# The four RWKV pairs of a hybrid block side by side, in units of two chunks

## The chip, the cores and the metric

The kernel runs on one core of a Trainium2 chip. The metric is the device time of one execution in microseconds (us). The times of the kernel before are the median, the least and the greatest of three executions; the profile is from a further execution of the same program. Five engines work side by side and wait for each other by semaphores: TensorE (PE; its weight loads are listed as PEld), VectorE (DVE), ScalarE (ACT), GpSimd (POOL) and SyncE (SP), which here issues most loads and stores.

## The reference, cut to what matters

The block is feed-forward network, mixer, feed-forward network on 1024 tokens of width 1024, all in fp32. The mixer adds four heads of gated linear attention (GLA) and eight heads of RWKV-7:

```python
x = x + 0.5 * swiglu(rms_norm(x, ffn1_norm), ffn1_w_gate, ffn1_w_up, ffn1_w_down)   # d_ff 2816
proj = rms_norm(x, mix_norm) @ w_in
o_gla  = gla_mixer(...)     # 4 heads, dk 64, dv 128, chunks of 64
o_rwkv = rwkv7_mixer(...)   # 8 heads of 64
x = x + concatenate([o_gla, o_rwkv]) @ w_out
x = x + 0.5 * swiglu(rms_norm(x, ffn2_norm), ffn2_w_gate, ffn2_w_up, ffn2_w_down)
return rms_norm(x, final_norm)

def rwkv_step(state, inp):              # lax.scan over the tokens, for every head
    r_t, w_t, k_t, v_t, a_t, b_t = inp
    sa = einsum('bhvk,bhk->bhv', state, a_t)
    state = state * w_t + sa * b_t + v_t * k_t       # outer products of v and k
    return state, einsum('bhvk,bhk->bhv', state, r_t)
# then: group norm over each head, * ln_w + ln_b, + (sum(r*k*r_k) * v), * g
```

## The kernel before, in words

**Tiling and stages.** The tokens are two halves, A and B, of 512. Each half goes through first network, projection, mixers, output projection `pout` and second network. Every large fp32 product is three matmuls on pieces of 128x512: the weights are loaded into `raw`, ScalarE makes the rounded part `wH` (L452) and VectorE the rest `wL` (L453), and TensorE adds high by high, high by low and low by high.

**The mixers** of a half have many small, dependent matmuls. So their matmuls are interleaved with large ones of the other half's networks, the "filler": tiles `pgu` (gate and up) and `pdn` (down). `mixers()` (from L1211) writes TensorE's order by hand. Each piece of mixer work is a generator that issues its instructions up to a `yield` with an estimate of how long its result takes (table `LAT`, times `SLACK`); until that much work was issued on TensorE, fillers are issued. Between the mixers' last matmuls and `pout` stands what is left of the filler's share. The other engines work in the order in which their instructions were issued.

**RWKV.** Two heads make a pair, which fills 128 partitions; there are four pairs, and eight chunks of 64 tokens in a half. `rwkv_duo` (L49) does two pairs:
- preparation, for all eight chunks at once: load `AR` and `BK` (L62, L65), gram matmuls `pg`, masked into `WA` and `W` (L83); then the inverse of a triangular matrix by 15 triples of VectorE operations on the tile `lb` and `R` (L105 to L107), its transpose `D` (L114), matmuls `p` with `D`, `p1b`, `p`, `p2b`, and `pav`;
- the chunk loop, eight steps, each dependent on the one before: `pz`, `Z`, `pu`, `UV`, `px`, new state `X`, and the output `py`;
- the norm of all eight chunks, transposes `pyT` (L47), eight ScalarE operations (L238), two loads, and a store to the scratch `d_mix` (L242).

The second duo begins after the first one's loop. GLA is done for two heads at a time by `gla_unit` (L244): loads `cum`, `k`, `q`, `kN`, `qx`, `vN` (L252, L254), matmuls `pkv`, levels `pA` and `pB`, and `po`. The first GLA unit may start when the first duo has its loads, the second when the first is done and the duo's loop begins.

**After the mixers** `outprep` loads all of `d_mix` into `xnL` (L1271), ScalarE makes the high part `xnH` (L1272), and `pout` begins.

Of the kernel before, what the change touches and what calls it, by code (L numbers as in the profile page):

```python
# [48 lines left out]
def rwkv_duo(g, d, src, mixout):  # L49


    nc=g.nc; V,S,T,GP=nc.vector,nc.scalar,g.T,nc.gpsimd
    C=g.C; vec=g.vec
    QS=range(2); PS=[2*d,2*d+1]
    mt=lambda shape,tag,nm,**kw: g.mx.tile([128]+shape,F32,tag=tag,name=nm,**kw)
    ps=lambda nm: g.pa.tile([128,512],F32,tag="pa",name=nm)
    def ld(nm,q):
        t=mt([512],"s2",nm); nc.sync.dma_start(t,src[q][nm]); return t
    AR=[mt([2,8,64],"AR","AR") for q in QS]
    BK=[]  # L60
    for q in QS:
        nc.sync.dma_start(AR[q].rearrange("p x c t->p (x c t)"),src[q]["AR"])  # L62
        for i in range(2):
            BK.append(mt([4,2,64],"s2","BK"))
            nc.sync.dma_start(BK[-1].rearrange("p c y t->p (c y t)"),src[q]["BK"][:,512*i:512*i+512])  # L65
    pc=[g.pc[p] for p in PS]
    yield LAT["pre"]
    yield "A"

    fr=[slice(0,64),slice(64,128)]  # L70
    mg=C["mg"].rearrange("p (x t)->p x t",x=2)
    WA=[[mt([8,64],"WA","WA") for h in range(2)] for q in QS]
    W=[[mt([8,64],"W","W") for h in range(2)] for q in QS]
    for q in QS:
        for i in range(2):
            c4=slice(4*i,4*i+4)
            pg=[ps(f"pg{h}").rearrange("p (c x t)->p c x t",c=4,x=2) for h in range(2)]
            for c in range(4):
                for h in range(2):
                    T.matmul(pg[h][:,c],BK[2*q+i][fr[h],c].rearrange("p y t->p (y t)"),AR[q][fr[h],:,4*i+c,:],start=True,stop=True,tile_position=(64*h,0))  # L80
            for x,Wx in ((1,WA),(0,W)):
                for h in range(2):
                    V.tensor_tensor(Wx[q][h][:,c4],pg[h][:,:,x],mg[:,x:x+1,:].to_broadcast([128,4,64]),op=MULT)  # L83
            yield 0

    fl=lambda t: t.rearrange("p q c t->p (q c) t")
    c32=fl(mt([2,8,32],"i2","c32"))
    c32q=c32.rearrange("p (q c) t->p q c t",q=2)
    for q in QS:
        for h in range(2):  # L90
            for gg in range(2):
                rr=slice(64*h+32*gg,64*h+32*gg+32)
                S.copy(c32q[rr,q],WA[q][h][rr,:,32*gg:32*gg+32])
    c16=fl(mt([2,8,16],"s1","c16"))
    S.mul(c16,c32[:,:,0:16],C["mq0"])
    V.scalar_tensor_tensor(c16,c32[:,:,16:32],C["mq1"],c16,op0=MULT,op1=ADD)
    S.mul(c32[:,:,16:32],c32[:,:,16:32],C["mq0"])
    GP.memset(c32[:,:,0:16],0.0)
    R16=fl(mt([2,8,16],"s1","R16"))
    V.tensor_copy(R16,C["i16"].rearrange("p (o t)->p o t",o=1).to_broadcast([128,16,16]))  # L100
    yield LAT["c32"]
    for j in range(15):
        n=15-j
        lb=mt([16,n],"lb","lb",bufs=2,padded_shape=[128,16,16])
        V.stream_shuffle(lb,c16[:,:,j+1:16],[j]*16+[16+j]*16)  # L105
        V.tensor_tensor(lb,lb,R16[:,:,j:j+1].to_broadcast([128,16,n]),op=MULT)
        V.tensor_tensor(R16[:,:,j+1:16],R16[:,:,j+1:16],lb,op=ADD)  # L107
        if j%2: yield LAT["inv2"]-40*j

    R4=mt([2,8,32],"Rd","R"); R=fl(R4)  # L110
    S.mul(R[:,:,0:16],R16,C["mq0"])
    S.mul(R[:,:,16:32],R16,C["mq1"])
    D=fl(mt([2,8,32],"i2","D"))
    V.transpose(D.rearrange("p c t->p (c t)"),R.rearrange("p c t->p (c t)"))  # L114
    yield LAT["D"]
    qd=[slice(32*i,32*i+32) for i in range(4)]
    p1=ps("p1").rearrange("p (c t)->p c t",t=32)
    for c in range(16):
        for i,r in enumerate(qd):
            T.matmul(p1[r,c],c32[r,c,:],D[r,c,:],start=True,stop=True,tile_position=(32*i,32*i))  # L120
    X1=fl(mt([2,8,32],"i2","X1"))
    S.copy(X1,p1)
    yield LAT["m1"]
    p1=ps("p1b")[:,0:256].rearrange("p (c t)->p c t",t=16)
    for c in range(16):
        for i,r in enumerate(qd):
            T.matmul(p1[r,c],X1[r,c,:],R[r,c,16:32],start=True,stop=True,tile_position=(32*i,32*i))
    V.tensor_tensor(R[:,:,16:32],p1,R[:,:,16:32],op=ADD)
    D=mt([2,8,32],"i2","D2")
    V.transpose(D.rearrange("p q c t->p (q c t)"),R.rearrange("p c t->p (c t)"))  # L130
    yield LAT["m2"]
    yield "B"
    half=[(slice(64*h,64*h+32),slice(64*h+32,64*h+64)) for h in range(2)]
    R64=mt([2,8,64],"R64","R64")
    S.mul(fl(R64)[:,:,0:32],R,C["mg0"])
    S.mul(fl(R64)[:,:,32:64],R,C["mg1"])
    p2=ps("p2").rearrange("p (q c t)->p q c t",q=2,c=8)
    for q in QS:
        for c in range(8):
            for h,(ra,rb) in enumerate(half):  # L140
                T.matmul(p2[rb,q,c,:],WA[q][h][ra,c,32:64],D[ra,q,c,:],start=True,stop=True,tile_position=(64*h,64*h+32))
    X2=mt([2,8,32],"i2","X2")
    for ra,rb in half:
        S.copy(X2[rb],p2[rb])

    WN=[[mt([8,64],"WN","WN") for h in range(2)] for q in QS]
    UV=mt([2,8,2,64],"UV","UV")
    for q in QS:
        for h in range(2):
            nc.sync.dma_start(WN[q][h].rearrange("p c d->p (c d)"),src[q][f"wn{h}"])  # L150
            kr=slice(64,128) if h==0 else slice(0,64)
            nc.sync.dma_start(UV[kr,h,:,q,:],src[q]["vt"][kr].rearrange("p (c d)->p c d",c=8))
    idn=C["idn"]
    yield LAT["x2"]
    p2=ps("p2b").rearrange("p (q c t)->p q c t",q=2,c=8)
    for q in QS:
        for c in range(8):
            for h,(ra,rb) in enumerate(half):
                T.matmul(p2[ra,q,c,:],X2[rb,q,c,:],R4[rb,q,c,:],start=True,stop=True,tile_position=(64*h+32,64*h))
    for ra,rb in half:  # L160
        S.copy(R64[ra,:,:,32:64],p2[ra])
    yield LAT["pav"]
    AV=mt([8,2,64],"AV","AV")
    for q in QS:
        pav=ps("pav")
        for c in range(8):
            for h in range(2):
                kr=slice(64-64*h,128-64*h)
                T.matmul(pav[fr[h],64*c:64*c+64],WA[q][h][kr,c,:],UV[kr,h,c,q,:],start=True,stop=True,tile_position=(64-64*h,64*h))
        S.copy(AV[:,:,q,:],pav.rearrange("p (c d)->p c d",c=8))  # L170
    yield "P"
    yield LAT["w"]

    YS=AV
    X=[g.X[p] for p in PS]
    two=lambda t: t[:,0:128].rearrange("p (q d)->p q d",q=2)
    def yout(c,X):
        py=two(ps("py"))
        for q in QS:
            for h in range(2):  # L180
                T.matmul(py[fr[h],q],AR[q][fr[h],0,c,:],X[q][fr[h]],start=True,stop=False,tile_position=(64*h,64*h))
            for h in range(2):
                T.matmul(py[fr[h],q],W[q][h][:,c,:],UV[:,h,c,q,:],start=False,stop=True,tile_position=(0,64*h))
        S.copy(YS[:,c],py)
    for c in range(8):
        pz=two(ps("pz"))
        for q in QS:
            for h in range(2):
                T.matmul(pz[fr[h],q],AR[q][fr[h],1,c,:],X[q][fr[h]],start=True,stop=True,tile_position=(64*h,64*h))
        Z=mt([2,64],"Z","Z",bufs=2); V.tensor_tensor(Z,pz,AV[:,c],op=ADD)  # L190
        if c: yout(c-1,Xo)
        yield LAT["z"]
        pu=two(ps("pu"))
        for q in QS:
            for h in range(2):
                T.matmul(pu[fr[h],q],R64[fr[h],q,c,:],Z[fr[h],q],start=True,stop=True,tile_position=(64*h,64*h))
        V.tensor_copy(UV[0:64,0,c],pu[0:64])
        S.copy(UV[64:128,1,c],pu[64:128])
        XP=[mt([64],"XP","XP",bufs=2) for q in QS]
        for q in QS: S.mul(XP[q],X[q],pc[q][:,c:c+1])  # L200
        yield LAT["u"]
        px=two(ps("px"))
        for q in QS:
            for h in range(2):
                T.matmul(px[fr[h],q],WN[q][h][:,c,:],UV[:,h,c,q,:],start=True,stop=True,tile_position=(0,64*h))
        Xn=[mt([64],"X","Xn",bufs=4) if c<7 else g.st.tile([128,64],F32,tag=f"X{p}",name="Xe",bufs=2) for p in PS]
        for q in QS: V.scalar_tensor_tensor(Xn[q],px[:,q],pc[q][:,c:c+1],XP[q],op0=MULT,op1=ADD)
        Xo=X; X=Xn
# [1327 lines left out]
```

## Time and profile before

| | us |
|---|---|
| median of 3 executions | 2178.34 (2177.96 to 2182.11) |
| profiled execution | 2179.36 |
| its span | 2177.5 |
| its mean granted clock of TensorE | 0.979 |
| mixer stage of half A, from the first filler behind the projection to `pout` | 745.59 to 1021.40 |
| mixer stage of half B | about 1292.8 to 1568.1 |

An engine's busy time is the sum of its instructions; the idle time ahead of an instruction is put down to what released it. The granted clock is given as a share of full speed. Times along the rows are us from the start of the span, durations of single instructions are ns where the heading of the view says so.

### The profile page before, as it was taken

The numbers are of one execution on the slowest core, as the hardware profiler recorded it, in microseconds if no ns is written. First come the engines' busy times: TensorE is split into PE (matmuls) and PEld (weight loads), VectorE is DVE, ScalarE is ACT, GpSimd is POOL, SyncE is SP. The second block draws the span as 40 slices with busy tenths as digits, with TensorE's granted clock in tenths as the row PEclk, the third lists the DMA queues.
The fourth block names the chain that finished last, engine by engine and source line by source line (L and its number), as shares of the span: only waits on it lengthen the run. The fifth ranks groups of instructions, "written<-read, shape, count | busy, mean of one in ns | idle before, by whom it ended". The sixth has DMA issues, their size and how long they took to land.

```text
span 2177.5 us, 36074 instructions
## 1 busy us (share of the span) xinstructions
PE 2069.3 (95%) x13588; PEld 1643.8 (75%) x13588; DVE 1436.5 (66%) x2771; ACT 912.9 (42%) x1723; POOL 468.6 (22%) x489
## 2 busy tenths in 40 slices
PE   8999999979999989997999999999799999998998
PEld 7778788767788877675878887777587778876886
DVE  6665687739569575665475957566558557876755
ACT  5432233322556444343265645434344223432243
POOL 0410355445012200000001220001103035445400
PEclk9999999989999999999999999999899999998999
DMA  5333244666455823334236673333434333459542
GB/s 190 126 119 95 102 146 150 249 261 216 149 190 195 274 75 112 127 99 154 94 125 198 196 266 90 111 126 105 168 104 145 100 109 123 173 178 353 180 141 77
DMA packets 152286, 336.81 MB, mean 155 GB/s; under 512 B 25616, under 2 KB 27696, under 8 KB 152112
## 3 DMA queue, kind: packets, MB, share of 16 engines
q1 hardware_dynamic: 126976, 250.08, 35.0%
q0 software_dynamic: 21536, 73.41, 9.2%
q10 hardware_dynamic: 3600, 11.01, 1.4%
q8 instruction: 107, 1.75, 0.3%
q14 instruction: 67, 0.55, 0.1%
HBM read 242.17 MB, written 92.27 MB: 154 GB/s over the span
## 4 chain that ended last, share of the span: by engine, by line
PE 86%; DVE 5%; DMA 3%; issue 2%; ACT 2%; POOL 1%; SPq 0%; ACTq 0%; POOLq 0%; DVEq 0%
PE pgu L44 22%; PE pju L44 17%; PE pdn L44 13%; PE pp L44 11%; PE pjd L44 6%; PE pout L44 4%; PE pv L44 2%; PE py L44 1%; PE po L44 1%; DVE x L888 1%; DVE wL L453 1%; PE pt L47 1%; PE pz L44 1%; PE ptn L47 1%; PE pg L44 1%
## 5 line engine op out<-in xcount | busy, mean ns | idle before, releaser
L453 DVE TENSOR_TENSOR wL<-raw,wH 128x512 fp32r<-128x512 f32 (+1 forms) x430 | 301.0, 708 | 280.7 <-ACT wH L452 272.8
L452 ACT CAST wH<-raw 128x512 fp32r<-128x512 f32 (+1 forms) x430 | 264.0, 619 | 464.4 <-PE pgu L44 146.4
L44 PE MATMUL pgu<-xnL,wH 128*128 128x512 f32 (+1 forms) x784 | 309.9, 396 | 0.0
L44 PE MATMUL pgu<-xnH,wH 128*128 128x512 f32 (+1 forms) x784 | 308.3, 394 | 0.0
L44 PE MATMUL pgu<-xnH,wL 128*128 128x512 f32 (+1 forms) x784 | 307.8, 393 | 0.2 <-DVE wL L453 0.2
L44 PE MATMUL pju<-T,wH 128*128 128x512 f32 x640 | 201.3, 396 | 2.4 <-ACT wH L688 2.4
L44 PE MATMUL pjd<-wH,hh 128*128 128x512 f32 x528 | 172.8, 408 | 20.9 <-ACT wH L688 20.9
L44 PEld LDWEIGHTS pgu<-xnL,wH 128*128 128x128 f32 x784 | 147.8, 189 | 33.4 <-issue 0.3
L44 PEld LDWEIGHTS pgu<-xnH,wH 128*128 128x128 f32 x784 | 147.7, 189 | 33.2 <-ACT xnH L511 0.7
L44 PEld LDWEIGHTS pgu<-xnH,wL 128*128 128x128 f32 x784 | 147.8, 189 | 32.4 <-DVE wL L453 0.4
L44 PE MATMUL pdn<-wH,hH 128*128 128x512 f32 x384 | 157.6, 412 | 8.1 <-DVE hf L661 4.5
L44 PE MATMUL pdn<-wL,hH 128*128 128x512 f32 x384 | 157.9, 412 | 1.9 <-DVE wL L453 1.9
L44 PE MATMUL pdn<-wH,hL 128*128 128x512 f32 x384 | 157.6, 411 | 1.5 <-issue 1.3
L624 DVE SCALAR_TENSOR_TENSOR x<-pdn,x 128x512 f32<-128x512 f32 x152 | 104.2, 688 | 73.2 <-PE pdn L44 71.7
L44 PEld LDWEIGHTS pju<-T,wH 128*128 128x128 f32 x640 | 120.2, 188 | 31.5 <-ACT wH L688 3.3
L44 PE MATMUL pp<-xnH,wH 128*128 128x512 f32 x352 | 140.8, 400 | 0.0
L44 PE MATMUL pp<-xnL,wH 128*128 128x512 f32 x352 | 139.2, 395 | 0.0
L44 PEld LDWEIGHTS pjd<-wH,hh 128*128 128x128 f32 x528 | 103.8, 197 | 46.2 <-ACT wH L688 21.8
L44 PE MATMUL pp<-xnH,wL 128*128 128x512 f32 x352 | 138.7, 394 | 0.0
L44 PE MATMUL pju<-T,wL 128*128 128x512 f32 x320 | 126.0, 394 | 0.0
L44 PE MATMUL pjd<-wL,hh 128*128 128x512 f32 x264 | 108.0, 409 | 6.6 <-DVE wL L689 6.6
L44 PEld LDWEIGHTS pdn<-wH,hH 128*128 128x128 f32 x384 | 73.9, 192 | 29.9 <-DVE hf L661 6.1
(395 smaller groups left out, 4104.5 us busy)
## 6 DMA issues: line engine op xcount, KB each, us to landing
raw<-in_wgu_dram SPq DMA_DIRECT2D x272, 256.0 KB, 2.7
hh<-d_hid SPq DMA_DIRECT2D x66, 512.0 KB, 4.6
d_hid<-hh POOLq DMA_DIRECT2D x62, 512.0 KB, 3.8
raw<-in_wdn_dram SPq DMA_DIRECT2D x96, 256.0 KB, 2.7
raw<-in_win_t_dram SPq DMA_DIRECT2D x88, 256.0 KB, 3.0
d_x<-x SPq DMA_DIRECT2D x20, 512.0 KB, 2.6
wdk<-in_wdn_dram SPq DMA_DIRECT2D x20, 512.0 KB, 8.4
raw<-in_w_out_dram SPq DMA_DIRECT2D x32, 256.0 KB, 2.6
```

The source lines that it names most:

```text
L44: return self.t.matmul(out,lhsT,rhs,**kw)
L47: return self.t.transpose(out,in_,idn)
L452: S.copy(H, raw)
L453: V.tensor_tensor(L, raw, H.bitcast(F32), op=SUB)
L624: V.scalar_tensor_tensor(h.x[tt][:, co], ps, 0.5, h.x[tt][:, co], op0=MULT, op1=ADD)
L888: V.scalar_tensor_tensor(x, v, k, x, op0=MULT, op1=ADD)
```

## The change

`rwkv_duo` is replaced by a class `Quad`. It cuts the eight chunks of a half into four units of two chunks and works on all four pairs in each. Three generators, for preparation, loop and norm, run as streams of their own: the loop of a unit waits for the tag `P` of its preparation, the norm for the tag `L` of its loop, and the preparation of unit u for `L` and `N` of unit u-2. GLA is a fourth stream, which does both units one after the other and waits for no tag. The tiles keep their sizes with other axes (8 blocks: 4 pairs x 2 chunks) except those of the inverse, which have 8 blocks in place of 16. The scratch tensors `AR`, `BK`, `bv`, `g`, `vt`, `wn` and the RWKV part of `mix` now hold the four pairs side by side. The state of the four pairs is one tile: `Xt = px + X`, `Xn = Xt * pc`. The table `LAT` and some buffer counts change.

```diff
-LAT=dict(pre=4444,c32=1600,inv2=1750,D=1500,...,w=2115,z=1400,u=1350,x=1650,gn=14000,gpre=2635,...)
+LAT=dict(pre=3000,gram=0,c32=3000,inv2=1400,D=900,...,w=600,z=1000,u=1000,x=1500,gn=6000,gpre=2635,...)
+class Quad:
+    def prep(self):
+        for u in range(4):
+            if u>1: yield f"?L{u-2}"
+            to=slice(128*u,128*u+128)
+            AR=mt([8,128],"AR","AR")
+            nc.sync.dma_start(AR,src["AR"].rearrange("p q x t->p (q x) t")[:,:,to])
+            BK=mt([4,256],"BK","BK")
+            nc.sync.dma_start(BK,src["BK"][:,:,256*u:256*u+256])
...
+            for j in range(15):
+                n=15-j
+                lb=mt([8,n],"lb","lb",bufs=2,padded_shape=[128,8,16])
+                V.stream_shuffle(lb,c16[:,:,j+1:16],[j]*16+[16+j]*16)
+                V.tensor_tensor(lb,lb,R16[:,:,j:j+1].to_broadcast([128,8,n]),op=MULT)
+                V.tensor_tensor(R16[:,:,j+1:16],R16[:,:,j+1:16],lb,op=ADD)
+                if j%2: yield LAT["inv2"]
...
+            yield f"P{u}"
+    def loop(self):
+        for u in range(4):
+            yield f"?P{u}"
+            for c in range(2):
+                pz=four("pz")
...
+                Z=mt([4,64],"Z","Z",bufs=1); V.tensor_tensor(Z,pz,AV[:,c],op=ADD)
+                yield LAT["z"]
...
+                V.tensor_copy(UV[0:64,0,:,cs],pu[0:64])
+                S.copy(UV[64:128,1,:,cs],pu[64:128])
+                yield LAT["u"]
...
+                Xt=mt([4,64],"Xt","Xt",bufs=1); V.tensor_tensor(Xt,px,X,op=ADD)
+                V.tensor_tensor(Xn,Xt,pc,op=MULT)
...
+                S.copy(AV[:,c],py)
+                yield LAT["x"]
+            yield f"L{u}"
+    def norm(self):
+        for u in range(4):
+            yield f"?L{u}"
...
+            nc.sync.dma_start(src["mix"][:,:,to],o)
+            yield f"N{u}"
-BUFS = dict(s2=7, W=4, WA=4, WN=4, AR=2, s1=2, i2=3, g1=3)
+BUFS = dict(s2=7, W=4, WA=2, WN=4, AR=2, UV=2, AV=2, R64=2, s1=2, i2=3, g1=3, s3=2)
-        def allowed(s):
-            if s in L:
-                return "A" in R[0].tags if s is L[0] else L[0].done and "P" in R[0].tags
-            return s is R[0] or "Q" in R[0].tags
+        todo = [Stream(x) for x in (quad.loop(), quad.prep(), quad.norm(), both_gl())]
```

SyncE's queue at the start of half A's mixers, the loads of the first RWKV work and of the first GLA unit. Before:

```order
L62 DMA AR<-d_AR_0_5600 128x1024
L65 DMA BK<-d_BK_0_5612 128x512 x2
L62 DMA AR<-d_AR_0_5780 128x1024
L65 DMA BK<-d_BK_0_5792 128x512 x2
L252 DMA cum<-d_la_0_5448 128x512
L252 DMA k<-d_kk_0_6412 128x512
L252 DMA q<-d_q_0_6351 128x512
L254 DMA vN<-d_vn_5369 128x4x256
L252 DMA kN<-d_kN_0_6592 128x512
```

The same place in the changed kernel:

```order
L69 DMA AR<-d_AR_5591 128x8x128
L72 DMA BK<-d_BK_5603 128x4x256
L260 DMA cum<-d_la_0_5439 128x512
L260 DMA k<-d_kk_0_6385 128x512
L260 DMA q<-d_q_0_6325 128x512
L260 DMA kN<-d_kN_0_6562 128x512
L260 DMA qx<-d_qx_0_6328 128x512
L262 DMA vN<-d_vn_5363 128x4x256
L452 DMA raw<-in_wdn_dram 128x512 x2
```

One `AR` and one `BK` for all four pairs stand there now in place of two `AR` and four `BK` for two; `kN` and `qx` moved ahead of `vN`. On TensorE the first `pkv` stood behind 40 fillers and four groups of `pg`; it now stands behind 19 fillers alone.

TensorE at the end of half A's mixers, from the fillers ahead of the last `pyT` to `pout`. Before:

```order
L44 MATMUL pgu<-xnH,wH 128x512
L47 MATMUL pyT<-ct,AV 128x128 x8
L44 MATMUL pgu<-xnL,wH 128x512
L44 MATMUL pgu<-xnH,wL 128x512
L44 MATMUL pgu<-xnH,wH 128x512
L44 MATMUL pgu<-xnL,wH 128x512
L44 MATMUL pgu<-xnH,wL 128x512
L44 MATMUL pout_10205<-wH,xnH 128x512
```

The same place in the changed kernel, where the left-out rows are more of the same fillers, 49 in all:

```order
L43 MATMUL pdn<-wL,hH 128x512
L46 MATMUL pyT<-ct,AV 128x128 x4
L43 MATMUL pdn<-wH,hL 128x512
L43 MATMUL pgu<-xnH,wH 128x512
L43 MATMUL pgu<-xnL,wH 128x512
L43 MATMUL pgu<-xnH,wL 128x512
...
L43 MATMUL pout_10238<-wH,xnH 128x512
```

The last transposes are four, of one unit, and stand 49 fillers ahead of `pout` and not five. Over the whole mixer stage of a half the counts are the same, 648 fillers and 1344 mixer matmuls; the fillers stand in 63 separate runs and stood in 82.

## Rows read from the trace of the kernel before

**Rows 1.** The page: busy time of each engine, and the group of `wL`
```profile
PE 2069.3 (95%) x13588; PEld 1643.8 (75%) x13588; DVE 1436.5 (66%) x2771; ACT 912.9 (42%) x1723; POOL 468.6 (22%) x489
...
L453 DVE TENSOR_TENSOR wL<-raw,wH 128x512 fp32r<-128x512 f32 (+1 forms) x430 | 301.0, 708 | 280.7 <-ACT wH L452 272.8
```

**Rows 2.** Waits of PE: reader, releaser, total us, number, longest
```profile
PE pout L44 <- ACT xnH L1272: 22.4, 2, 11.4
...
PE p L44 <- DVE D L114: 7.0, 3, 3.0
```

**Rows 3.** Windows: stretch, length; PE, PEld, DVE, ACT, POOL busy; clock, DMA, GB/s
```profile
745.50:1021.50 276.00, 254.76 (x3307) 190.20 (x3305) 171.29 (x492) 121.05 (x248) 2.12 (x4) 0.97 0.38 118
1292.80:1568.10 275.30, 254.39 (x3306) 190.07 (x3305) 174.56 (x492) 120.97 (x247) 17.12 (x19) 0.98 0.38 121
761.00:783.00 22.00, 21.98 (x305) 16.75 (x307) 21.45 (x85) 13.99 (x27) 0.31 (x1) 1.00 0.44 102
783.00:788.00 5.00, 1.95 (x50) 1.35 (x44) 4.93 (x20) 1.54 (x3) 0.00 (x0) 1.00 0.18 50
1022.00:1024.00 2.00, 2.00 (x6) 1.58 (x5) 2.00 (x4) 1.80 (x4) 0.00 (x0) 0.50 1.05 397
1800.00:1900.00 100.00, 100.00 (x431) 80.85 (x430) 81.99 (x98) 39.64 (x70) 56.17 (x52) 1.00 0.44 156
```

**Rows 4.** Timeline of PE, 832 to 839: start, duration, instruction
```profile
832.80 0.50 PE L44 MATMUL pgu<-xnH,wH 128*128 128x512 f32 x1
...
835.31 0.45 PE L44 MATMUL pu<-Z,R 64*64 64x64 f32 x8
835.68 0.50 PE L44 MATMUL pgu<-xnL,wH 128*128 128x512 f32 x1
...
838.18 0.45 PE L44 MATMUL px<-UV,WN 128*64 128x64 f32 x8
```

**Rows 5.** Timeline of PE, start and end of half A's stage
```profile
745.59 0.39 PE L44 MATMUL pgu<-xnH,wH 128*128 128x512 f32 x1
...
759.98 1.09 PE L44 MATMUL pkv<-vN,kN 128*64 128x128 f32 x16
...
1008.11 1.06 PE L47 MATMUL pyT<-ct,AV 128*128 128x128 f32 x8 [0.32 <-DVE AV L226]
...
1021.40 0.80 PE L44 MATMUL pout<-wH,xnH 128*128 128x512 f32 x1 [11.06 <-ACT xnH L1272]
```

**Rows 6.** Timeline of SP's DMA issues, start and end of the stage
```profile
744.58 0.44 SPq L62 DMA_DIRECT2D AR<-d_AR  x1
...
750.27 0.55 SPq L254 DMA_DIRECT2D vN<-d_vn  x1
...
1012.63 3.20 SPq L242 DMA_DIRECT2D d_mix<-AV  x2
...
1016.42 0.94 SPq L1271 DMA_DIRECT2D xnL<-d_mix  x2
```

**Rows 7.** Timeline of ACT after the last `pyT`
```profile
1008.82 4.34 ACT L238 ACTIVATE AV<-pyT,vt 64x256 f32<-64x256 f32 x8 [2.23 <-PE pyT L47]
```

**Rows 8.** DMA issues, 744 to 760: count, KB each, us to landing
```profile
vN<-d_vn SPq DMA_DIRECT2D x1, 512.0 KB, 8.4
...
UV<-d_vt SPq DMA_DIRECT2D x1, 128.0 KB, 5.9
```

**Rows 9.** Groups of DVE by shape, 745 to 1022: busy us, mean ns, idle
```profile
L83 DVE TENSOR_TENSOR WA<-pg,ct 128x256 f32<-128x256 f32 x16 | 6.1, 419 | 3.3 <-PE pg L44 3.3
...
L105 DVE STREAM_SHUFFLE lb<-c 128x128 f32<-128x128 f32 x2 | 0.6, 308 | 0.0
...
L105 DVE STREAM_SHUFFLE lb<-c 128x64 f32<-128x64 f32 x2 | 0.5, 242 | 0.0
...
L106 DVE TENSOR_TENSOR lb<-lb,R 128x64 f32<-128x64 f32 x2 | 0.4, 220 | 0.0
L107 DVE TENSOR_TENSOR R<-R,lb 128x64 f32<-128x64 f32 x2 | 0.4, 218 | 0.0
```

More of the change, by code (lines that the diff above doesn't have):

```diff
@@ L7 @@
 MULT,ADD,SUB,MAX,MIN=ALU.mult,ALU.add,ALU.subtract,ALU.max,ALU.min
-LAT=dict(pre=4444,c32=1600,inv2=1750,D=1500,m1=1200,m2=1200,D2=1300,x2=600,pav=900,w=2115,z=1400,u=1350,x=1650,gn=14000,gpre=2635,lev0=5723,lev=1944,sc=770,on=8372)
-SEQ_MID=3
+LAT=dict(pre=3000,gram=0,c32=3000,inv2=1400,D=900,m1=900,m2=900,x2=700,pav=900,w=600,z=1000,u=1000,x=1500,gn=6000,gpre=2635,lev0=5723,lev=1944,sc=770,on=8372)
 def const_array():
@@ L47, in transpose @@
         return self.t.transpose(out,in_,idn)
[L49 to L78, printed above, removed]
-                for h in range(2):
-                    T.matmul(pg[h][:,c],BK[2*q+i][fr[h],c].rearrange("p y t->p (y t)"),AR[q][fr[h],:,4*i+c,:],start=True,stop=True,tile_position=(64*h,0))
-            for x,Wx in ((1,WA),(0,W)):
-                for h in range(2):
[L83 to L208, printed above, removed]
-        if c==SEQ_MID: yield "M"
-        yield LAT["x"] if c<7 else 0
-    yout(7,Xo)
-    yield "Q"
-    for q,p in enumerate(PS): g.X[p]=X[q]
-    c16_=YS.rearrange("p c q t->p (c q) t")
-    b16=lambda t: t.rearrange("p (c o)->p c o",o=1).to_broadcast([128,16,64])
-    sm=mt([16],"sm","sm",bufs=2)
-    V.tensor_reduce(sm,c16_,axis=AX.X,op=ADD)
-    V.tensor_scalar(sm,sm,-1.0/64,None,op0=MULT)
-    V.tensor_tensor(c16_,c16_,b16(sm),op=ADD)
-    vr=mt([16],"sm","vr",bufs=2)
-    for i in range(2):
-        sq2=mt([8,64],"s2","sq2"); S.activation(sq2,c16_[:,8*i:8*i+8],AF.Square)
-        V.tensor_reduce(vr[:,8*i:8*i+8],sq2,axis=AX.X,op=ADD)
-    g.rsqrt(g.mx,vr,vr,64,64e-5)
-    V.tensor_tensor(c16_,c16_,b16(vr),op=MULT)
-    yield LAT["gn"]
-    pyv=[]
-    for i in range(2):
-        py=ps("pyT")
-        for j in range(4): T.transpose(py[:,128*j:128*j+128],YS[:,4*i+j].rearrange("p q d->p (q d)"),idn)
-        pyv.append(py.rearrange("p (c h t)->p c h t",c=4,h=2))
-    yT=YS.rearrange("p c q t->p (c q t)").rearrange("p (q c t)->p q c t",q=2,c=8)
-    for q,p in enumerate(PS):
-        for h in range(2):
-            lw,lb_=("ln_w","ln_b") if h==q else ("ln_ws","ln_bs")
-            for i in range(2):
-                S.activation(yT[fr[h],q,4*i:4*i+4,:],pyv[i][fr[q],:,h,:],AF.Identity,scale=vec(lw,p)[fr[q]],bias=vec(lb_,p)[fr[q]])
-        o=yT[:,q].rearrange("p c t->p (c t)")
-        bv=ld("bv",q); V.tensor_tensor(o,o,bv,op=ADD)
-        gt=ld("g",q); V.tensor_tensor(o,gt,o,op=MULT)
-        nc.sync.dma_start(mixout[q],o)
@@ L270, in gla_unit @@
     D=g.mx.tile([128,2,4,32],F32,tag="D32",name="D32")
-    pA=[ps(f"pA{h}") for h in range(2)]
     def lev(h):
@@ L288, in gla_unit @@
     qe,ke=e64
+    pA=[ps(f"pA{h}") for h in range(2)]
     for h in range(2):
@@ L291, in gla_unit @@
             T.matmul(pA[h][0:64,64*c:64*c+64],ke[fr[h],64*c:64*c+64],qe[fr[h],64*c:64*c+64],start=True,stop=True,tile_position=(64*h,0))
-    yield 0
     qe,ke=e32
@@ L313, in gla_unit @@
         for h in range(2):
-            if h: yield 0
             for c in range(4):
@@ L330, in gla_unit @@
     for h in range(2):
-        if h: yield 0
         for c in range(4):
@@ L373 @@
 NH, NL, NR = 6, 6, 4
+WIDE = {f"{n}{p}": (n, p) for n in ("AR", "BK", "bv", "g", "vt") for p in range(4)} | {f"wn{p}{i}": (f"wn{i}", p) for p in range(4) for i in range(2)}
 class Pool:
@@ L425, in block_kernel @@
     GP.memset(carry, 0.0)
-    g.X, g.S, g.pc, g.el = [], [], {}, {}
-    for i in range(4):
-        t = wk.tile([P, 64], F32, tag=f"X{i}", bufs=2, name="X0")
-        GP.memset(t, 0.0)
-        g.X.append(t)
+    g.S, g.el = [], {}
+    g.X = wk.tile([P, 4, 64], F32, tag="X", bufs=2, name="X0")
+    GP.memset(g.X, 0.0)
     for i in range(2):
@@ L940, in dn @@
         def dn(nm, cols=HT):
-            return dram(f"{nm}_{hf}", [P, cols])
+            nm, p = WIDE.get(nm, (nm, None))
+            if p is None:
+                return dram(f"{nm}_{hf}", [P, cols])
+            return dram(f"{nm}_{hf}", [P, 4 * cols])[:, cols * p:cols * p + cols]
         def put(nm, t, cols=HT):
@@ L1074, in proj @@
                 S.activation(Em, cs, AF.Exp, scale=CDEC)
-                pc = wk.tile([P, 8], F32, tag=f"pc{p}", name="pc")
-                V.tensor_copy(pc, E[:, :, 64])
-                g.pc[p] = pc
+                if p == 0:
+                    g.pc = wk.tile([P, 4, 8], F32, tag="pc", bufs=2, name="pc")
+                V.tensor_copy(g.pc[:, p], E[:, :, 64])
                 r = shifted(f"r{p}", new("r"))
@@ L1213, in mixers, with wide @@
         d = lambda nm, cols=HT: dram(f"{nm}_{hf}", [P, cols])
-        def rw(k):
-            return rwkv_duo(g, k, [{n: d(f"{n}{p}", 2 * HT if n in ("AR", "BK") else HT) for n in ("AR", "BK", "vt", "bv", "g")} | {f"wn{i}": d(f"wn{p}{i}") for i in range(2)} for p in (2 * k, 2 * k + 1)],
-                            [d(f"mix{4 + p}") for p in (2 * k, 2 * k + 1)])
+        def wide(nm, cols=HT):
+            return dram(f"{nm}_{hf}", [P, 4 * cols]).rearrange("p (q t)->p q t", q=4)
+        quad = Quad(g, {n: wide(n) for n in ("bv", "g", "vt", "wn0", "wn1", "mix")} |
+                    {"BK": wide("BK", 2 * HT), "AR": wide("AR", 2 * HT).rearrange("p q (x t)->p q x t", x=2)})
         def gl(p):
@@ L1222, in gl @@
                             [d(f"go{2 * p + j}") for j in range(2)], [d(f"mix{2 * p + j}") for j in range(2)])
+        tags = set()
         class Stream:
             def __init__(self, gen):
-                self.gen, self.at, self.tags, self.done = gen, T.ns, set(), False
+                self.gen, self.at, self.wait, self.done = gen, T.ns, None, False
             def step(self):
-                self.tags.add("started")
                 try:
                     lat = next(self.gen)
-                    if isinstance(lat, str):
-                        self.tags.add(lat)
-                        lat = 0.0
+                    while isinstance(lat, str) and lat[0] != "?":
+                        tags.add(lat)
+                        lat = next(self.gen)
+                    self.wait, lat = (lat[1:], 0.0) if isinstance(lat, str) else (None, lat)
                     self.at = T.ns + lat * SLACK
@@ L1237, in step, with free, both_gl @@
                     self.done = True
-        R = [Stream(rw(k)) for k in range(2)]
-        L = [Stream(gl(p)) for p in range(2)]
-        def allowed(s):
-            if s in L:
-                return "A" in R[0].tags if s is L[0] else L[0].done and "P" in R[0].tags
-            return s is R[0] or "Q" in R[0].tags
-        todo = R + L
+            def free(self):
+                return self.wait is None or self.wait in tags
+        def both_gl():
+            for p in range(2):
+                yield from gl(p)
+        todo = [Stream(x) for x in (quad.loop(), quad.prep(), quad.norm(), both_gl())]
         filling = True
@@ L1253, in mixers @@
                     break
-                can = [s for s in todo if allowed(s)]
+                can = [s for s in todo if s.free()]
                 t0, n = T.ns, 1
@@ L1270, in outprep @@
             raw = h.xl(kt).bitcast(F32)
-            nc.sync.dma_start(raw, dram(f"mix{kt}_{h.i}", [P, HT]))
+            nc.sync.dma_start(raw, dram(f"mix{kt}_{h.i}", [P, HT]) if kt < 4 else dram(f"mix_{h.i}", [P, 4 * HT])[:, HT * kt - 4 * HT:HT * kt - 3 * HT])
             S.copy(h.xh(kt), raw)
```

155 lines of the change are left out of this document (added).

## The prediction

> **What bounds the kernel now.** I read the page first: TensorE is busy for 95% of the span, VectorE for 66%, ScalarE for 42% [rows 1]. The median of the runs shown is 2178.34 us; the profiled execution took 2179.36, its span 2177.5. Every duration below is from that execution, so the sum starts at 2179.36, and at the end I take off the 1.0 us by which it stands above the median.
>
> The change touches only the two mixer stages, so I looked at those by windows. Half A's stage takes 276.0 us with 254.76 of them busy on TensorE, half B's 275.3 with 254.39 [rows 3]. Idle are thus 21.2 and 20.9, together 42.1 us, and more than this no better order of the same work could win except by making the work itself cheaper. The waits of TensorE split it: `pout`, the output projection, waited twice for `xnH`, 22.4 us in all and 11.4 at most [rows 2]; the remaining 19.8 lie inside the stages.
>
> Where the inside waits come from is seen in two short stretches: from 761 to 783 us VectorE is busy for 21.45 of 22 us and TensorE has work all the time; from 783 to 788 VectorE is busy for 4.93 of 5 and TensorE for 1.95 [rows 3]. There TensorE has run out of what the hand-written order put ahead of the products `p` with `D`, the end of a triangular inverse that VectorE works out in 45 small operations; it is the wait of up to 3.0 us, 7.0 in three, of rows 2.
>
> **The change, part by part.** The instructions of TensorE stay the same in number: 648 filler matmuls of the other half's feed-forward network and 1344 small mixer matmuls in a half, before and after; only their order differs.
>
> *Fewer switches.* A pure filler stretch sustains 431 matmuls in 100 us at full clock, with TensorE busy throughout [rows 3], so one each 0.232 us. Ten filler matmuls between two mixer groups took 2.51 us (832.80 to 835.31, and 2.50 from 835.68 to 838.18) [rows 4], where 10 x 0.2315 is 2.32: each separate run of fillers costs about 0.2 us more than its matmuls. The order of before has 82 such runs in a half, the new one 63, so 38 fewer in the two halves: 38 x 0.2 = **-7.6 us** (0 if the extra time belongs to the small matmuls and not to the switch, -11 if 0.3 is lost with the groups' own ends).
>
> *The wait of `pout`.* Before, the last eight transposes `pyT` run at 1008.11 and only five fillers are left behind them. ScalarE takes 4.34 us for eight operations, the store `d_mix` follows at 1012.63, the loads `xnL` are issued at 1016.42, and `pout` starts at 1021.40 after 11.06 us of waiting [rows 5, 6, 7]. In the new order the last `pyT` group has four transposes, of a unit of two chunks, and 49 fillers stand behind it: 49 x 0.2315 + 0.2 = 11.5 us of cover. The path itself takes 1021.40 - 1008.11 = 13.3 before; ScalarE's eight operations have the same number but 128 columns in place of 256, which by the ratio of smaller operations in rows 9 (242 against 308) makes them 4.34 x 0.79 = 3.4, so the path is about 12.4. A wait of 0.9 us is left each time: 22.4 - 1.8 = **-20.6 us**. After the wait the granted clock was 0.50, the lower of the two levels of 1.2 and 2.4 GHz; six matmuls started in 2 us, where the 431 in 100 make 8.6 [rows 3]. That cost 2.6 x 0.23 = 0.6 us in these 2; how long it lasted the row doesn't say. Between one such stretch and four it is 0.6 to 2.4 us in a half; I take the upper part, since `pout` is followed by 192 dense matmuls that had to bring the clock back: **-4 us** for both halves (-1 to -5).
>
> *The inside waits.* VectorE's work grows by the inverse: it was 15 triples (shuffle, multiply, add) on 16 blocks, twice in a half; it is 15 triples on 8 blocks, four times. At 128x64, the size in the middle of the new ones, a triple cost 242 + 220 + 218 = 680 ns [rows 9], so a unit's inverse takes 15 x 0.68 = 10.2 us. It now lies beside loop steps and GLA of other units in place of filler alone: from a unit's last gram matmuls `pg` to its `p` the new order gives TensorE (in fillers x 0.2315 plus groups) 43, 46, 30 and 24 us in units 0 to 3. For VectorE I count there, from the new order by these rows with `wL` at 708 ns [rows 1], 27 to 30, 34, 25 and 20 to 23 us. Three units have cover, the last is at the edge. So most of the 19.8 us should go; I keep 2.5 in each half for the last unit and its two loop steps, which have only three or four fillers between dependent groups: 19.8 - 5 = **-15 us** (from 0 to -19.8).
>
> *What is late next: the start.* GLA's stream now runs from the first moment, and its `pkv` stands behind 19 fillers, not behind four `pg` groups and 40. The stage begins at 745.59, so TensorE reaches `pkv` at 745.59 + 19 x 0.2315 + 0.2 = 750.2. `pkv` needs `vN`. Before, `vN` was issued at 750.27 and took 8.4 us, to 758.7, and `pkv` ran at 759.98 [rows 5, 6, 8], with no wait. Up to and with `vN`, SyncE's queue held two `AR` of 512 KB, four `BK` of 256, `cum`, `k`, `q` of 256 and `vN` of 512, in all 3.25 MB, and these took from 744.58 to 758.7, 14.1 us. In the new order one `AR` and one `BK` of 512 KB stand there, and `kN` and `qx` beside `cum`, `k`, `q`: 2.75 MB. In proportion that is 2.2 us less, so `vN` lands between 756.5 and 758.7 (nothing gained, since the new `AR` rows are short, of 512 bytes); I take 757.3. TensorE then waits 7 us in A and, with the same order and loads, about 6.5 in B; everything else waits behind `pkv` on TensorE's queue, the fillers too. Then the clock: after 11 us of waiting it was 0.50, so I add 1.75 each. In all **+17 us** (0 if `vN` comes before TensorE, +22 if it lands no earlier than before and the clock costs 2.4 each).
>
> What short rows do is bounded by the old `UV` load, 128 KB with rows of 256 bytes, landing in 5.9 us, where whole-row loads of 512 KB took 8.4 [rows 8]: nothing strange is seen. The Trainium skill (DMA: Bandwidth & Descriptors, section Specifications) puts the least transfer at line rate at 512 bytes; by this rule the new rows are just long enough, `vN` lands at the earlier end, and the sum is 2 us lower. No row here shows a transfer of 512-byte rows.
>
> The wait is what the Trainium skill warns of (TensorE: Matmul & The Clock Gate, section HAM oscillation — how this bites in real kernels): a wait for a transfer leaves TensorE idle, and its next work begins at the slower clock. The trace agrees with 0.50 behind `pout`. By the rule the 3.5 us for the clock are in the sum; had the clock stayed full it would be 2144.5.
>
> *The rest.* The state update becomes two VectorE operations of 256 columns in place of one multiply on ScalarE and one on VectorE for each pair; a 128x256 operation from PSUM costs 419 ns [rows 9]; it is within the counts above. Uncovered, 16 steps x 0.42 are 7 us. `BK` has one buffer now, so the next unit's load waits for the `pg` of the unit before; 160 fillers (37 us) lie between the two units' `pg` in the new order, so it costs nothing, or, if SyncE's queue is held by it and the weights behind it come late, one wait of some 8 us, the landing time of `vN`. Stores to the wide scratch have the same bytes. I cost all three at nothing.
>
> **Sum.** -7.6 - 20.6 - 4 - 15 + 17 = -30.2: 2179.4 - 30.2 = 2149.2, and 2148 against the median.
>
> **Rivals.**
> - *VectorE stays the bound inside the stages.* The inverses are interleaved with steps, and the row 761 to 783 shows how full VectorE can be. Against: 66% of the span, and the counts above. The 15 us don't come: 2163.
> - *The end still waits.* The path from `pyT` to `pout` passes one SyncE queue, on which other loads stand (`raw` of `w_out` among them), and the loads `xnL` wait for all stores; if this takes as long as before in spite of 49 fillers, through a store or a load that is issued late, 20.6 + 4 stay: 2172. For it: the old path had 3.8 us between store and loads [rows 6].
> - *The start costs nothing.* `vN` and `kN` come with the lighter queue, or the stage's fillers hold TensorE longer: 2131.
> - *Slower.* The small operations of a loop step (`Z`, `UV`, `Xt`, `Xn`) queue behind inverse triples on VectorE, which works in order. Three of the dependent operations in each of 8 steps in both halves make 48 places. If each waits for one triple of 0.68 us with nothing else for TensorE to do, it is 48 x 0.68 = 33 us, just what the change wins, so this decides from one triple for each. With a `wL` of 0.71 as well it is 48 x 1.39 = 67: 2149 + 67 = 2215. Against: five to eight fillers (1.2 to 1.9 us) stand between most dependent groups.
> - *It doesn't do what it says:* TensorE has as many matmuls as before and is 95% full; what is won at the end is lost at the start. 2178.
>
> **How the numbers follow.** Forecast 0.50, its own range 2136 to 2160; VectorE bound inside 0.21; end still waits 0.11; start free 0.07; slower 0.07; nothing 0.04. Within 0.2%, 4.4 us, is what a measurement of this kernel can tell from no change. Faster: the first four, less a part of the third that falls into that band (0.04): 0.85. Same: 0.04 + 0.04 = 0.08. Slower 0.07. The range from 2130 to 2172 holds the forecast, the second and third rival, and most of the fourth.
>
> **What would show it.** Right: `pout` waits about 1 us in place of 11, the clock behind it at 1.00; `pkv` waits some 7 us near 750 and again 4.6 us after the start of B's stage, with 0.50 behind it; waits of TensorE for `D` and others inside the stages under 3 us a half; both stages near 260 us. Wrong: a stage with VectorE at 95% or more over 20 us while TensorE waits; `pout` waiting for a load; a `pkv` that runs at once; waits spread over `pz`, `pu`, `px` in the middle of the stage, which is the slower case.

## The result, and the profile after

The changed kernel takes 2147.85 us in the median of four executions (2144.43 to 2152.21); the ratio to the kernel before is 0.985, 95% interval 0.9823 to 0.9878. The forecast was 2148 us. The profiled execution is the slowest of the four, 2152.21 us with a span of 2150.4, so everything read from its trace explains a gain of 27.1 us of span (2177.5 - 2150.4), not the 32 between the medians.

The page's first line stands beside the one of [rows 1]:

```profile
PE 2056.5 (96%) x13588; PEld 1643.0 (76%) x13588; DVE 1451.6 (68%) x3031; ACT 910.6 (42%) x1703; POOL 469.0 (22%) x490
```

TensorE's matmuls are as many as before; its busy time is 12.8 us less, for the same work. (The trace lists most of the mixers' matmuls as two records each, so the 3306 of a stage are the 648 fillers and the 1344 mixer matmuls.) The windows of the two mixer stages, and behind them stretches just after a wait (columns as in [rows 3]):

```profile
744.50:1006.10 261.60, 249.40 (x3306) 190.87 (x3304) 177.49 (x619) 119.16 (x236) 3.27 (x7) 0.99 0.41 123
1277.70:1542.30 264.60, 251.88 (x3306) 192.76 (x3304) 178.96 (x619) 119.19 (x236) 7.56 (x11) 0.97 0.41 122
756.20:760.20 4.00, 3.96 (x21) 3.10 (x21) 1.88 (x6) 0.59 (x1) 0.00 (x0) 0.50 1.17 236
1290.30:1296.30 6.00, 6.00 (x37) 4.73 (x37) 1.88 (x6) 2.57 (x4) 0.00 (x0) 0.50 1.23 242
1306.60:1310.00 3.40, 3.40 (x19) 2.69 (x9) 3.40 (x14) 3.22 (x8) 0.00 (x0) 0.50 0.02 7
1006.00:1008.00 2.00, 1.95 (x5) 1.39 (x6) 1.98 (x4) 1.64 (x4) 0.00 (x0) 0.56 0.95 324
1542.30:1544.30 2.00, 2.00 (x8) 1.34 (x9) 2.00 (x4) 1.64 (x4) 0.61 (x1) 1.00 0.93 282
```

The first two stretches stand behind `pkv` in A and B, the third behind a wait of 1.0 us of GLA's `pA` in B, and the last two behind `pout` in A, where the clock is 0.56, and in B, where it is 1.00. Stage A is 14.4 us shorter than in [rows 3], stage B 10.7. Idle are 12.2 and 12.7 us, and the waits of TensorE say where (total us, number, longest):

```profile
PE pkv L43 <- DMA vN<-d_vn: 15.1, 2, 7.9
...
PE pA L43 <- DVE ke L289: 3.3, 4, 1.0
PE pout L43 <- ACT xnH L1285: 3.0, 2, 1.9
...
PE pout L43 <- DVE xnL L1286: 0.6, 1, 0.6
PE p L43 <- DVE D L130: 0.5, 2, 0.2
```

`pout` waits 3.0 us and not 22.4 [rows 2]; the wait for the inverse's `D`, 7.0 before, is 0.5; a new one stands at the top, `pkv` for `vN`, 15.1. The timeline of TensorE at both ends of half A's stage, beside [rows 5], and `pkv` of half B:

```profile
756.24 1.98 PE L43 MATMUL pkv<-vN,kN 128*64 128x128 f32 x16 [7.12 <-DMA vN<-d_vn]
...
992.20 0.60 PE L46 MATMUL pyT<-ct,AV 128*128 128x128 f32 x4
...
1006.05 0.64 PE L43 MATMUL pout<-wH,xnH 128*128 128x512 f32 x1 [1.87 <-ACT xnH L1285]
...
1290.26 1.97 PE L43 MATMUL pkv<-vN,kN 128*64 128x128 f32 x16 [7.95 <-DMA vN<-d_vn]
```

SyncE's issues in the same places, beside [rows 6], and ScalarE and VectorE after the last `pyT`, beside [rows 7]:

```profile
743.60 0.61 SPq L69 DMA_DIRECT2D AR<-d_AR  x1
...
998.55 0.57 SPq L249 DMA_DIRECT2D d_mix<-AV  x1
999.21 1.06 SPq L452 DMA_DIRECT2D raw<-in_w_out_dram  x2
1000.31 3.68 SPq L1284 DMA_DIRECT2D xnL<-d_mix  x7
```

```profile
992.83 3.72 ACT L244 ACTIVATE AV<-pyT,vt 64x128 f32<-64x128 f32 x8 [0.28 <-PE pyT L46]
...
997.84 0.69 DVE L248 TENSOR_TENSOR AV<-AV,g 128x512 f32<-128x512 f32 x1
...
1005.38 0.62 ACT L1285 CAST xnH<-xnL 128x512 fp32r<-128x512 f32 x1 [3.56 <-DMA xnL<-d_mix]
```

The path from the last `pyT` to `pout` did not get shorter: 1006.05 - 992.20 = 13.9 us, and 13.3 before. Two lines of the trace of before show why, the last store and the first use of the loads:

```profile
1015.51 0.33 SPq L242 DMA_DIRECT2D d_mix<-AV  x1
...
1020.73 2.65 ACT L1272 CAST xnH<-xnL 128x512 fp32r<-128x512 f32 x4 [6.40 <-DMA xnL<-d_mix]
```

The store is now issued 6.4 us after `pyT`, as VectorE's last operation on the tile ends (997.84 + 0.69); of the two stores of before the last went 7.4 us after `pyT`. Behind it the gain is lost: the loads `xnL` follow 1.8 us after the store, where they followed 0.9 after the last one, with two weights of `w_out` between them on SyncE's queue; and ScalarE starts on the first of them 5.1 us after its issue, where it took 4.3. What covers the path now is the 49 fillers.

### The profile page after: what moved, and what is told of

The parts are those of the page before. It is cut to its first block, busy times and chain, and to the rows that moved or that the text cites. A ratio compares the mean times of both kernels' runs of the same rounds, so it can differ in the third digit from the quotient of the medians.

```text
span 2150.4 us, 36294 instructions
## 1 busy us (share of the span) xinstructions
PE 2056.5 (96%) x13588; PEld 1643.0 (76%) x13588; DVE 1451.6 (68%) x3031; ACT 910.6 (42%) x1703; POOL 469.0 (22%) x490
## 5 line engine op out<-in xcount | busy, mean ns | idle before, releaser
L460 DVE TENSOR_TENSOR wL<-raw,wH 128x512 fp32r<-128x512 f32 (+1 forms) x430 | 296.5, 697 | 277.7 <-ACT wH L459 275.4
L696 DVE TENSOR_TENSOR wL<-s,wH 128x512 fp32r<-128x512 f32 x80 | 68.3, 855 | 42.5 <-ACT wH L695 42.5
```

The lines of the kernel that those rows point to most:

```text
L460: V.tensor_tensor(L, raw, H.bitcast(F32), op=SUB)
L696: V.tensor_tensor(L, f, H.bitcast(F32), op=SUB)
```

## The experiments

Ratios are to the kernel before, measured on the same chip with the runs; the changed kernel's is 0.985. Each has an interval of about 0.0025 to either side, 5 to 6 us, so differences of two runs below that are said from the traces or left open.

**The end by itself: the kernel before with more cover.**

```diff
-    run(f1b, n=3)      # and f2a for the other half
+    run(f1b, n=4)
```

> The kernel before with 48 more fillers of each half between its last transposes and the output projection, 53 in place of 5; everything else as before. Theory (the end's gain is cover alone and does not need the units of two chunks): pout's wait of 22.4 us falls to about 2, and with the clock behind it 22 to 24 us are won: about 2157 us, two thirds or more of what the whole change wins. Rival (only a shorter last unit shortens the path, and fillers moved ahead are missed behind pout): 2170 us or more.

2162.82 us, ratio 0.9919 (0.9893 to 0.9944). The wait of `pout` in this kernel:

```profile
PE pout L44 <- ACT xnH L1272: 5.2, 2, 3.7
```

17.2 of the 22.4 us are gone without any of the units, and about half of the whole change's gain comes with one number. The waits for `D` stay: 6.1 us. The first theory is nearer, but its two thirds are missed: 5.2 us of the wait are left, not 2, and a slow clock still follows, with 46.4 us for the 192 matmuls of `pout` in each half, where it was 46.0 and 47.3.

**The end of the changed kernel with the same edit.**

> The changed kernel with 48 more fillers of each half between the last transposes and the output projection, 97 in all. Theory (the rest of the end wait, 1.9 and 1.2 us, and the slow clock behind it, 1.7 and 1.3 us, are due to too little cover): both go, 5 to 6 us less, about 2142 us. Rival (the fillers are missed where they stood before, behind the output projection): the same wait comes back there, 2147 us, no change.

2138.07 us, ratio 0.981 (0.9785 to 0.9834), some 9 us less than the changed kernel, more than the 5 to 6 of the theory. `pout` waits no longer, and its 192 matmuls (counted from the first start to the last, and one step of 0.23 more) take 44.5 and 44.4 us, where they took 46.2 and 45.8. The fillers are not missed behind it. The stages' windows, used below:

```profile
741.10:1011.90 270.80, 260.05 (x3354) 199.93 (x3353) 185.24 (x631) 125.30 (x247) 3.27 (x7) 0.99 0.44 132
1270.60:1541.30 270.70, 259.90 (x3353) 199.91 (x3352) 185.98 (x629) 125.49 (x247) 7.88 (x11) 0.99 0.43 128
```

**The start: GLA's first products later.**

```diff
-    yield LAT["gpre"]
+    yield LAT["gpre"] if p else 9500
```

> Only the first GLA unit's estimated latency is changed (2635 to 9500), so that its first products stand behind 55 fillers and the first gram products, not behind 19 fillers. Theory (the new wait for vN, 7.1 and 7.9 us, and about 1.9 us of slow clock behind each, is a term of its own): the wait goes and nothing takes its place, 15 to 19 us less than the changed kernel, about 2130 us. Rival (VectorE is near its limit, so GLA's levels collide with unit 0's inverse when they come later): waits of TensorE for D, ke or UV inside the stages grow by as much as the start wins, 2142 to 2150 us.

2143.99 us, ratio 0.9833 (0.9809 to 0.9858): only some 4 us, not clear of the noise. The wait for `vN` is gone, and these stand in its place:

```profile
PE p L43 <- DVE D L115: 8.2, 4, 2.7
...
PE pg L43 <- DMA BK<-d_BK: 3.4, 2, 2.1
...
PE pB L43 <- issue: 2.5, 1, 2.5
```

```profile
840.00:852.00 12.00, 9.93 (x208) 7.60 (x206) 11.57 (x54) 10.08 (x24) 0.00 (x0) 1.00 0.21 67
```

```profile
913.01 3.71 ACT L244 ACTIVATE AV<-pyT,vt 64x128 f32<-64x128 f32 x8
916.74 0.40 ACT L112 ACTIVATE R<-R,ct 128x128 f32<-128x128 f32 x1
...
916.75 0.69 DVE L248 TENSOR_TENSOR AV<-AV,bv 128x512 f32<-128x512 f32 x1 [3.89 <-ACT AV L244]
```

In the 12 us before the first of these `p`, the second unit's, VectorE is busy for 11.57: there GLA's work falls onto the inverse, as the rival says, and the wait is 1.4 us in each half. The larger waits, 2.6 us in A and 2.7 in B, are the third unit's and have another cause. VectorE sits idle for 3.89 us before it, since ScalarE works on the norm of the unit before, and the two operations on `R` that `D` needs stand behind that norm's eight in ScalarE's order. So the rival's time came, but at most 2.8 of the 8.2 us by its mechanism. From this run I formed a new theory, that the wait at the start could not be won at all, and tried it without touching TensorE's order.

**The start: `vN` and `kN` loaded first.**

```diff
-    cum=ld("cum"); k=ld("k"); q=ld("q"); kN=ld("kN"); qx=ld("qx")
-    vN=...; nc.sync.dma_start(vN,...)
+    vN=...; nc.sync.dma_start(vN,...)
+    kN=ld("kN")
+    if p==0: yield "V"
+    cum=ld("cum"); k=ld("k"); q=ld("q"); qx=ld("qx")
...
+        next(todo[3].gen)      # issues these two ahead of AR and BK
```

> The changed kernel, TensorE's order untouched, with the first GLA unit's loads of vN and kN issued ahead of AR and BK; cum, k and q come 0.75 MB later. First theory (the wait of pkv is a price of its own): 13 to 19 us less, about 2131 us. Theory formed after gla_later (the start is bound by all the loads and by VectorE's work on them, and the wait only shows where TensorE meets it first): pkv runs at once or nearly so, and pg, pA and p wait together about as long as pkv did; 2142 to 2149 us.

2134.71 us, ratio 0.9797 (0.977 to 0.9825), by the ratios 11.5 us less than the changed kernel (13 by the medians). The new theory fell, the first one stands, at the lower edge of its range: most of the wait is a price of its own.

```profile
747.31 1.09 PE L43 MATMUL pkv<-vN,kN 128*64 128x128 f32 x16
751.03 1.16 PE L43 MATMUL pg<-AR,BK 64*128 64x128 f32 x16 [1.27 <-DMA BK<-d_BK]
...
762.20 0.32 PE L43 MATMUL pA<-qe,ke 64*32 64x32 f32 x4 [2.07 <-DVE ke L291]
```

`pkv` runs at once, and 3.3 us of waits for `BK` and `ke` remain in A, where `pkv` and `pA` waited 8.1. In both halves together the waits for `vN`, `BK` and `ke` fall from 18.4 to 7.4 us.

**VectorE's cover.**

```diff
                 V.stream_shuffle(lb,c16[:,:,j+1:16],[j]*16+[16+j]*16)
+                V.stream_shuffle(lb,c16[:,:,j+1:16],[j]*16+[16+j]*16)
```

> The changed kernel with each of the 15 shuffles of every inverse done twice (the second writes the same values again), about 15 x 0.24 = 3.6 us more for VectorE in each of eight units. Theory (units 0 to 2 have cover, unit 3 is at the edge): only the last unit of each half pays, 0 to 7 us, 2148 to 2155 us, with the new wait at p with D in unit 3. Rival (VectorE bounds the stages everywhere): all of it is paid, 29 us, about 2177 us.

2157.62 us, ratio 0.9899 (0.9872 to 0.9925): some 10 us of the 29 that were added (eight units at 3.6).

```profile
PE pout L43 <- ACT xnH L1286: 9.0, 2, 4.5
...
PE p L43 <- DVE D L116: 6.6, 4, 2.2
```

Between the two, nearer the first. Units 0 and 1 hide it all; in half A unit 2's `p` waits 2.1 us and unit 3's 1.1, and the end 4.5, 2.6 more than before. I had given unit 2 five us to spare; it has less than 1.5.

**No preparation ahead.**

```diff
-            if u>1: yield f"?L{u-2}"
+            if u: yield f"?L{u-1}"
```

> The changed kernel, but a unit's preparation starts only when the loop of the unit before is done, so that the inverses no longer lie beside the loop steps (the norm still does). Theory (overlap of neighbouring units is what takes away the waits inside the stages): no filler is left for unit 3, whose whole chain of inverse, two steps and norm stands bare; 30 to 40 us of waits more in each half and slow clock with them, 2210 to 2240 us, more than before the change. Rival (the gain is from units of half the size and from the norm by units alone): within 15 us of the changed kernel, below 2165 us.

2229.5 us, ratio 1.0226 (1.019 to 1.0261), slower than the kernel before, as the theory said.

```profile
PE pout L43 <- ACT xnH L1285: 20.8, 2, 11.2
PE pyT L46 <- DVE AV L233: 19.4, 4, 6.8
```

```profile
1010.00:1046.00 36.00, 17.60 (x228) 13.88 (x227) 9.70 (x27) 7.65 (x18) 0.00 (x0) 0.50 0.11 33
```

The last unit's chain stands bare: in 36 us TensorE is busy for 17.60, all of it at half clock, and VectorE for 9.70. Units of two chunks are worth nothing without their overlap. The change also set new estimates in `LAT` for the order by hand; no run separates them from the units.

**The price of a switch.**

```diff
                     T.matmul(p1[r,c],c32[r,c,:],D[r,c,:],...)
+                if c==3: yield 0        # so too in p1b, p, p2b, pav and py; and n=4 at both ends
```

> The changed kernel with 48 more fillers at each half's end (as changed_more_tail, 2138 us) and further points at which fillers may stand between a unit's small matmuls: 85 separate runs of fillers in a half, not 63, with equal matmuls. Theory (each run costs 0.2 us): 44 more runs, 9 us more than changed_more_tail, about 2147 us, and about 4 us more of TensorE's busy time in each stage. Rival (the extra time belongs to the small matmuls, not to the switch): below 2141 us.

2155.03 us, ratio 0.9891 (0.9864 to 0.9919), 17 us more than with the runs unsplit, where the theory had 9.

```profile
742.60:1020.70 278.10, 266.22 (x3353) 199.09 (x3351) 183.46 (x624) 122.35 (x241) 3.27 (x7) 0.99 0.40 118
1279.70:1557.30 277.60, 265.59 (x3354) 198.97 (x3353) 184.62 (x625) 122.35 (x241) 7.59 (x11) 0.99 0.41 119
```

For equal matmuls TensorE is busy 6.2 and 5.7 us longer than in the windows of the kernel with more tail: 11.9 / 44 = 0.27 us for each run of fillers. The rest of the 17 is in waits (1.2 us more in each stage), in `pout` (0.3 each) and outside the stages.

**Both ends together.** The changed kernel with n=4 and the first GLA unit's estimate at 6000:

> Two edits of the changed kernel together: 48 more fillers at each half's end, and the first GLA unit's latency estimate at 6000, which puts its first products behind 31 fillers and the gram products. Theory (the start is bound by loads and VectorE): the gain of the end as in changed_more_tail and at most some 4 us from the start, 2133 to 2138 us. Rival (the start wait can still be won by finding the right place): about 2125 us.

2129.17 us, ratio 0.9771 (0.9743 to 0.9799): between the two, 4 us better than its theory.

```profile
PE p L43 <- DVE D L115: 2.0, 2, 1.0
...
PE pkv L43 <- DMA vN<-d_vn: 1.1, 2, 0.8
```

With 31 fillers ahead of `pkv` and not 55, the waits for `D` are 2.0 us in place of the 8.2 of gla_later, and `vN` costs 1.1. Against changed_more_tail it is 8 to 9 us less: the start can be won by place too. With n=4 and the loads of `vN` and `kN` first:

> The changed kernel with two edits: vN and kN loaded ahead of AR and BK, and 48 more fillers at each half's end. Theory (start and end are separate terms): 13 us for the start and 7 to 10 us for the end, 2125 to 2129 us. Rival (what the start wins, the end's fillers win too): 2131 us or more.

2127.79 us, ratio 0.9769 (0.9744 to 0.9794), 9 us less than changed_more_tail by the ratios: start and end add up within the noise, and loading first is worth no more here than the right place, from which it can't be told apart. Its stages are the cleanest look at the work itself:

```profile
742.40:1006.00 263.60, 258.36 (x3354) 198.62 (x3354) 185.29 (x631) 122.63 (x245) 3.27 (x7) 1.00 0.45 136
1264.60:1529.10 264.50, 258.19 (x3355) 198.52 (x3353) 185.92 (x630) 122.94 (x245) 7.89 (x11) 1.00 0.45 131
```

With `pA` put 7 fillers later on top of that:

> The same with the first GLA unit's latency estimate at 3600, not 2635, so that pA stands 7 fillers (1.6 us) later. Theory (what is left of the start wait is pA, which waits for VectorE's ke): pA's wait of 2 us in half A goes, 0 to 3 us less than the kernel without it. Rival (it collides with the inverse of unit 0, as in gla_later): p waits for D instead, no gain or up to 3 us more.

2133.12 us, ratio 0.9792 (0.9763 to 0.9822). It is some 5 us slower: its four executions, 2131.34 to 2141.5, all lie above those without it, 2125.02 to 2128.77, on the same chip. Neither theory names what the trace shows: the order now has `pg` ahead of `pkv`, and it waits for `BK`.

```profile
PE pg L43 <- DMA BK<-d_BK: 8.7, 2, 4.6
```

## Why the prediction was right

The mechanism was right in its four parts, and the median came out as forecast; the second is partly luck, since the terms missed in both directions and the trace explains 27 us, where the sum had 30. Inside the parts some steps failed, as said below. Term by term, in us for both halves, measured in the profiled executions:

| term | forecast | measured | from |
|---|---|---|---|
| fewer switches | -7.6 | -10.3 | 38 runs x 0.27 |
| slow clock behind the inside waits | 0 | -2.5 | 4.5 before, 2.0 after; see below |
| inside waits | -15 | -13.0 | 19.8 to 6.8 (24.9 idle - 15.1 - 3.0) |
| start, wait for `vN` | +13.5 | +15.1 | waits |
| slow clock behind it | +3.5 | +5.0 | 10 us of work at 0.50 |
| wait of `pout` | -20.6 | -19.4 | 22.4 to 3.0 |
| slow clock behind it | -4 | -2.6 | 192 matmuls, 44.45 at full clock: 46.0 + 47.3 before, 46.2 in A now |
| a second wait in `pout`, B | 0 | +1.3 | 45.8 at a clock of 1.00; 0.6 for `xnL`, the rest small gaps |
| sum | -30.2 | -26.4 | span: -27.1 |

The clock terms come out of the busy times. At a clock of 1.00 throughout, the new order's work takes 258.36 + 258.19 less 96 fillers of 0.2315, 494.3 us in both stages. The changed kernel was busy for 249.40 + 251.88 = 501.3: 7.0 more. Of these 5.0 are the half clock behind `pkv`, by the windows 4 us long in A and 6 in B, and 1.7 the 3.40 us at 0.50 from 1306.6 on; the table counts all but the 5.0 to the inside waits. The kernel before was busy for 509.15 [rows 3]: 14.8 more than the work, of which 10.3 are switches at the 0.27 of split_runs and 4.5 are left. Two windows of it that I had not looked at show half clock behind the inside waits, and would cost some 4 us:

```profile
790.00:796.00 6.00, 4.45 (x50) 3.58 (x50) 3.26 (x7) 1.60 (x3) 0.00 (x0) 0.51 0.11 37
1335.00:1339.00 4.00, 3.85 (x164) 3.54 (x165) 3.37 (x9) 1.85 (x3) 0.00 (x0) 0.57 0.51 149
```

**Switches.** Mis-sized: the 0.2 was read from one interval, and split_runs has 0.27. The upper bound named there, 0.3, was nearer; whether the rest is in the ends of the small groups isn't shown.

**The inside waits.** The step held, and preparation_not_ahead shows that it needs the overlap: without it the time comes back, as waits of the last unit. The missing term is the clock: a wait was priced as idle time alone.

**The end.** The step "the path is about 12.4" failed; it is 13.9. ScalarE's eight operations take 3.72, not 3.4, a ratio that was read from VectorE's rows. The rest is behind the store, which the forecast left as it was: two weights on SyncE's queue and slower loads, 1.6 us together. This is the second rival's mechanism in small, at 0.9 us, and not at 10. The 3.8 us between store and loads that spoke for this rival were misread: the row holds two stores, and 0.9 us lie between the last and the loads. That the clock would then stay up failed in half A, where it was 0.56 behind a wait of 1.87; in half B it stayed at 1.00 behind 1.15. The larger point is that the term was right and its cause wider than the change: cover alone gives most of it.

**The start.** The place held, and nearly the size: 7.1 and 7.9 us for a forecast of 7 and 6.5. In A `pkv` starts as `vN` lands, 756.2; it took 12.6 us from the first issue for 2.75 MB, 14.1 for 3.25 before: of the 2.2 us in proportion 1.5 came. In B nothing came. The first issue of the changed kernel, then of the kernel before the first issue, that of `vN`, and its time to landing:

```profile
1276.71 1.70 SPq L69 DMA_DIRECT2D AR<-d_AR  x1
...
1291.80 0.42 SPq L62 DMA_DIRECT2D AR<-d_AR  x1
...
1297.98 0.37 SPq L254 DMA_DIRECT2D vN<-d_vn  x1
...
vN<-d_vn SPq DMA_DIRECT2D x1, 512.0 KB, 6.8
```

The changed kernel takes 13.5 us to `pkv` at 1290.26, the kernel before 13.0 to the landing at 1304.8. By the Trainium skill's least transfer at line rate (DMA: Bandwidth & Descriptors, section Specifications) rows of 512 bytes should have brought all 2.2 in both halves, by my estimate; the trace agrees to 0.7 us in A and not at all in B, and doesn't say what the rest is.

**The rivals.** VectorE as the bound didn't come in this order, but it is not far: gla_later ran into it for at most 2.8 us, and changed_more_dve paid for a third of its added work. The slower rival, loop steps queued behind triples, was not seen: in the profile `pu` never waits for `Z`, and `px` once, for 0.4 us.

What stays open: the 0.7 us of span outside these terms, and why the profiled execution is the slowest of four.

## What to carry to other kernels

Before reordering for a wait at the end of a stage, try to put more independent work into it: here one number gave half of what a rewrite gave, and on top of the rewrite it gave 9 us more. When an order starts consumers earlier, put their loads in the order in which the consumers stand, or the consumers where their loads land: with the longer end, loading two tiles first and moving the consumers behind 31 fillers were worth some 9 us each, and moving them behind 55, without it, gave most of that away to waits for VectorE and ScalarE. Price a wait of TensorE with the slow clock that may stand behind it.
